# Channel scale and bias of the recurrence's output norm taken into the neighbouring operations

## The chip, the cores and the metric

The kernel runs on one core of a Trainium2 chip. The metric is the device time of one execution in microseconds. Several executions of the kernel before were timed; the profile shows one further execution.

## The reference, cut to what matters

The reference is a network of two layers. Each layer has a first feed-forward block, a mixer with three branches (a linear recurrence, a global and a windowed attention) and a second feed-forward block, on 256 tokens of 1024 channels, all in 32-bit floats. The change lies at the end of the recurrence's branch. There the sum `wkv` of the recurrence's two directions is normalized per head of 64 channels, scaled and shifted per channel, a bonus is added, and the result is multiplied with a gate:

```
mean = jnp.mean(wkv, axis=-1, keepdims=True)
var = jnp.mean(jnp.square(wkv - mean), axis=-1, keepdims=True)
y = ((wkv - mean) * lax.rsqrt(var + LNX_EPS)).reshape(bsz, s, RWKV_DIM) * lnx_g + lnx_b
y = y + bonus.reshape(bsz, s, RWKV_DIM)
gate = jax.nn.sigmoid(gl) @ g2
return y * gate
```

There are 8 heads of 64 channels, so 512 channels, and `lnx_g` and `lnx_b` have one value for each of them.

## The kernel before

One core does everything. Every weight matrix streams from HBM in units of 128x1024 floats (`unit`). Each unit is split into a high part `w_hi` (a rounding copy, line 62 on ScalarE or line 64 on VectorE) and a low part `w_lo` (a subtraction, line 93 on VectorE or GpSimd), and TensorE multiplies high with high, high with low and low with high (`mm3`, line 52). So nearly all of TensorE's time goes to weight matmuls, and the other engines work ahead of it.

The mixer consists of generators that each do a piece of work and then yield: the projections, the attention, the preparation of the recurrence, its four units (`wkv`, two halves of the heads by two directions), `post` and the output projections with their gates (`branches`). A string `ORDER`, written out by hand, tells which generator takes the next step; its letter O is `post`. Within this order the tile framework fills the queue of each engine. Another set of strings (`ENG`) picks the engine of single operations; the one for O is eight times v, VectorE.

`post` works on channels across partitions: a half of the heads is a tile `y` (`yacc`) of 128 channels by 2 pairs (`pp`) by 256 tokens, so 128x512. For each of the two halves it takes three steps. The first forms the product for the bonus (lines 974 and 975) and subtracts the mean (line 979). The second forms 1/rms per head and token (`head_rsqrt`: line 693 on VectorE, 694 on GpSimd, 696 on ScalarE). The third, which the change touches, spreads 1/rms over the channels with transposes into a PSUM bank `rb` (`hb` in the profile), multiplies `y` with it (line 985), applies the channel scale and bias from the columns `R_LG` and `R_LB` of the tile `par` (line 988, once for each `pp`), forms the bonus in a bank `bb` (`bonp`) and the gate in a bank `gb` (`gatep`) on TensorE, and then does on VectorE lines 995 (bonus times v), 996 (y plus bonus) and 997 (times gate). `split` follows: line 128 on ScalarE writes the high part of `yT`, line 130 on VectorE the low part. The output projection `wo` (lines 1044 and 1045 add its result up) multiplies with both parts. It comes soon after the third step of the second half; after that of the first half the units of the recurrence go on.

Of the kernel before, what the change touches and what calls it, by code (L numbers as in the profile page):

```python
# [11 lines left out]
ALU = mybir.AluOpType  # L12
# [16 lines left out]
class Net:  # L29
# [21 lines left out]
    def mm(self, *a, **k):  # L51
        return self.nc.tensor.matmul(*a, **k)  # L52
# [286 lines left out]
R_MU, R_W0, R_A0, R_KK, R_KA, R_RK, R_LG, R_LB, R_N = 0, 15, 23, 31, 35, 39, 43, 47, 51  # L339
# [16 lines left out]
class Mixer:  # L356
# [606 lines left out]
    def post(self):  # L963
        nc, n = self.nc, self.n
        V, mm = nc.vector, n.mm
        for hf in range(2):
            y, kas = self.ys[hf], self.unit[2 * hf][3]
            ps = slice(2 * hf, 2 * hf + 2)
            r, k, v = (self.RKV[:, i, ps, :] for i in range(3))
            pz = self.t([128, 4, 512], "pz", tag="Z", bufs=2)  # L970
            sq, bon = (pz[:, i].rearrange("p (a s) -> p a s", a=2) for i in (0, 1))
            for pp in range(2):
                p = 2 * hf + pp
                V.scalar_tensor_tensor(bon[:, pp, :], r[:, pp, :], self.par[:, R_RK + p:R_RK + p + 1], k[:, pp, :], ALU.mult, ALU.mult)
            self.pick("O").tensor_tensor(bon, bon, kas, ALU.mult)
            b = n.bank([128, 2, S], "mean")
            for pp in range(2):
                mm(b[:, pp, :], n.bones, y[:, pp, :], start=True, stop=True)
            V.tensor_tensor(y, y, b, ALU.subtract)
            nc.scalar.activation(sq, y, AF.Square)  # L980
            yield
            rb = self.head_rsqrt(sq, 2, 1.0 / 64, 64 * 1e-5, False, pz[:, 2])
            yield
            rb = rb()[0]
            V.tensor_tensor(y, y, rb, ALU.mult)
            for pp in range(2):
                p = 2 * hf + pp
                self.pick("O").tensor_scalar(y[:, pp, :], y[:, pp, :], self.par[:, R_LG + p:R_LG + p + 1], self.par[:, R_LB + p:R_LB + p + 1], ALU.mult, ALU.add)
            bb = n.bank([128, 2, S], "bonp")
            gb = n.bank([128, 2, S], "gatep")  # L990
            for pp in range(2):
                p = 2 * hf + pp
                mm(bb[:, pp, :], n.bones, bon[:, pp, :], start=True, stop=True)
                mm(gb[:, pp, :], self.g2[:, 128 * p:128 * p + 128], self.LG[:, 2, :], start=True, stop=True)
            V.scalar_tensor_tensor(bon, bb, 64.0, v, ALU.mult, ALU.mult)
            self.pick("O").tensor_tensor(y, y, bon, ALU.add)
            V.tensor_tensor(y, y, gb, ALU.mult)
            if hf == 0:
                self.ya = [self.t([128, 4, S], f"yT{i}", tag=f"yT{i}", bufs=2, dt=F32R) for i in range(2)]
            n.split(y, self.ya[0][:, ps, :], self.ya[1][:, ps, :])  # L1000
            yield
# [129 lines left out]
```

## Time and profile before

| what | us |
|---|---|
| median of 3 runs | 1452.02 |
| lowest and highest of them | 1450.62, 1454.06 |
| the profiled execution | 1456.31 |
| its span in the profile | 1454.4 |
| TensorE (PE) busy in the span | 1401.1 |
| VectorE (DVE) busy | 1004.6 |
| ScalarE (ACT) busy | 744.4 |
| GpSimd (POOL) busy | 206.2 |

PEld is the weight load of TensorE, which overlaps its matmuls. A line such as L93 is a line of the kernel. In the profile an operation reads as output<-inputs by the names of the tiles, with the shapes of the output and of the input that it goes over. A DVE instruction can start a little before the one ahead of it has ended, so distances between starts are shorter than durations where nothing has to be waited for.

### The profile page before, as it was taken

The page shows a single profiled execution, that of the slowest core. Times are in us where ns is not written, and L with a number is a line of the kernel's source. Part 1 is how long each engine was busy: PE and PEld are TensorE (multiplying, and loading weights), DVE is VectorE, ACT ScalarE, POOL GpSimd, SP SyncE. Part 2 cuts the span into 40 slices and gives each one's busy share as a digit, 9 for nine tenths or more (in the row PEclk, how much of TensorE's full clock was granted, in tenths as well). Part 3 has the DMA queues.
Part 4 walks back from the last instruction along what each step waited for, and adds up shares of the span by engine and source line. Part 5 has one row for each costly group of instructions (what it writes and reads, how often), then busy time and mean ns, then how long its engine had stood idle before and what let it go on. Part 6 is the DMA issues. An engine that isn't in the chain of part 4 may idle for free.

```text
span 1454.4 us, 25957 instructions
## 1 busy us (share of the span) xinstructions
PE 1401.1 (96%) x10482; PEld 1158.6 (80%) x10482; DVE 1004.6 (69%) x1518; ACT 744.4 (51%) x1241; POOL 206.2 (14%) x181
## 2 busy tenths in 40 slices
PE   7999999999998999999999999999998989999997
PEld 6888878877786878888888888788676868788886
DVE  5677467886867576776467864789758766668753
ACT  6555334665444355555455553356553443655543
POOL 0000033104315100000000000522041241000001
PEclk9999999999999999999999999999999999999999
DMA  7766656423314047666566666563243131576663
GB/s 219 209 201 187 195 152 190 130 70 120 113 50 144 27 144 205 189 191 194 162 188 196 190 192 191 159 182 100 67 132 102 49 114 48 167 207 188 189 191 112
DMA packets 113436, 220.24 MB, mean 151 GB/s; under 512 B 7362, under 2 KB 32164, under 8 KB 113316
## 3 DMA queue, kind: packets, MB, share of 16 engines
q1 hardware_dynamic: 111328, 215.08, 49.4%
q10 hardware_dynamic: 1508, 2.58, 0.5%
q8 instruction: 82, 1.34, 0.4%
q0 software_dynamic: 480, 0.93, 0.3%
q14 instruction: 38, 0.31, 0.1%
HBM read 217.51 MB, written 1.05 MB: 150 GB/s over the span
## 4 chain that ended last, share of the span: by engine, by line
PE 74%; DVE 8%; issue 8%; ACT 4%; DMA 3%; POOL 3%; SPq 0%; POOLq 0%; ACTq 0%; DVEq 0%
PE dn L52 19%; PE gt L52 18%; PE up L52 17%; PE gu L52 3%; PE wo L52 3%; PE rk L52 3%; DVE w_lo L93 2%; DMA w_raw<-in_w_in 2%; PE yp L52 1%; POOL w_lo L93 1%; PE Lp L52 1%; PE tp L55 1%; PE sc L52 1%; ACT w_hi L62 1%; DMA w_raw<-in_ffn_w_up 1%
## 5 line engine op out<-in xcount | busy, mean ns | idle before, releaser
L93 DVE TENSOR_TENSOR w_lo<-w_raw,w_hi 128x1024 fp32r<-128x1024 f32 (+1 forms) x360 | 444.1, 1234 | 252.0 <-ACT w_hi L62 248.5
L62 ACT ACTIVATE w_hi<-w_raw 128x1024 fp32r<-128x1024 f32 x358 | 379.8, 1062 | 403.4 <-PE dn L52 118.6
L52 PE MATMUL dn<-w_hi,aT 128*128 128x512 f32 x704 | 218.2, 390 | 0.0
L52 PE MATMUL gt<-hT,w_hi 128*128 128x512 f32 x512 | 179.0, 395 | 0.0
L52 PE MATMUL up<-hT,w_hi 128*128 128x512 f32 x512 | 178.2, 394 | 0.0
L52 PEld LDWEIGHTS dn<-w_hi,aT 128*128 128x128 f32 x704 | 131.9, 188 | 27.9 <-DVE sg L268 0.9
L93 POOL TENSOR_TENSOR w_lo<-w_raw,w_hi 128x1024 fp32r<-128x1024 f32 x50 | 123.5, 2474 | 149.4 <-ACT w_hi L62 91.1
L52 PE MATMUL gt<-hT,w_lo 128*128 128x256 f32 x512 | 142.2, 278 | 0.0
L52 PE MATMUL up<-hT,w_lo 128*128 128x256 f32 x512 | 141.8, 277 | 0.0
L52 PE MATMUL gt<-w_hi,hT 128*128 128x512 f32 x384 | 138.3, 421 | 0.0
L52 PE MATMUL dn<-w_lo,aT 128*128 128x512 f32 x352 | 137.7, 391 | 0.0
L52 PEld LDWEIGHTS up<-hT,w_hi 128*128 128x128 f32 x512 | 96.0, 188 | 22.3
L52 PEld LDWEIGHTS gt<-hT,w_hi 128*128 128x128 f32 x512 | 96.0, 188 | 22.1
L52 PEld LDWEIGHTS gt<-hT,w_lo 128*128 128x128 f32 x512 | 96.1, 188 | 0.2
L52 PEld LDWEIGHTS up<-hT,w_lo 128*128 128x128 f32 x512 | 96.1, 188 | 0.0
L52 PE MATMUL rk<-hT,w_hi 128*128 128x256 f32 x480 | 89.8, 288 | 4.0 <-DVE RKV L675 4.0
L52 PEld LDWEIGHTS gt<-w_hi,hT 128*128 128x128 f32 x384 | 73.0, 194 | 20.6 <-issue 5.2
L52 PEld LDWEIGHTS rk<-hT,w_hi 128*128 128x128 f32 x480 | 76.5, 194 | 6.9 <-DVE RKV L675 5.9
L52 PE MATMUL up<-w_hi,hT 128*128 128x512 f32 x256 | 81.4, 397 | 0.0
L52 PE MATMUL gt<-w_lo,hT 128*128 128x512 f32 x192 | 79.0, 411 | 0.0
L52 PEld LDWEIGHTS dn<-w_lo,aT 128*128 128x128 f32 x352 | 66.1, 188 | 14.8 <-DVE w_lo L93 1.4
L143 POOL TENSOR_SCALAR stat<-stat 128x1 f32<-128x1 f32 x14 | 3.4, 240 | 495.1 <-ACT gh L139 478.7
(272 smaller groups left out, 2427.9 us busy)
## 6 DMA issues: line engine op xcount, KB each, us to landing
w_raw<-in_ffn_w_up SPq DMA_DIRECT2D x160, 512.0 KB
w_raw<-in_w_in SPq DMA_DIRECT2D x102, 512.0 KB
w_raw<-in_ffn_w_down SPq DMA_DIRECT2D x88, 512.0 KB
w_raw<-in_ffn_w_up SPq DMA_DIRECT2D x32, 256.0 KB
w_raw<-in_w_out SPq DMA_DIRECT2D x16, 512.0 KB
w_raw<-in_w_o_ga SPq DMA_DIRECT2D x8, 512.0 KB
w_raw<-in_w_o_wa SPq DMA_DIRECT2D x8, 512.0 KB
w_raw<-in_w_o_rwkv SPq DMA_DIRECT2D x8, 512.0 KB
```

The costliest lines, as they stand in the source:

```text
L52: return self.nc.tensor.matmul(*a, **k)
L55: return self.nc.tensor.transpose(*a, **k)
L62: self.nc.scalar.activation(out, in_, AF.Copy, scale=1.0 if scale is None else scale)
L93: self.engine(on[1]).tensor_tensor(o, r, h.bitcast(F32), ALU.subtract)
L143: nc.gpsimd.tensor_scalar(self.ss[:, c:c + 1], self.ss[:, c:c + 1], 1.0 / D, EPS, ALU.mult, ALU.add)
```

## The change

The operation that multiplied the whole tile with 1/rms becomes two, one for each `pp`, which multiply with the channel's scale first and then with 1/rms. The bias is no longer added with the scale: the operation that added the bonus to the whole tile becomes two, which add the channel's bias and the bonus. The two operations of line 988 fall away. All new operations are on VectorE.

```
-            V.tensor_tensor(y, y, rb, ALU.mult)
             for pp in range(2):
                 p = 2 * hf + pp
-                self.pick("O").tensor_scalar(y[:, pp, :], y[:, pp, :], self.par[:, R_LG + p:R_LG + p + 1], self.par[:, R_LB + p:R_LB + p + 1], ALU.mult, ALU.add)
+                V.scalar_tensor_tensor(y[:, pp, :], y[:, pp, :], self.par[:, R_LG + p:R_LG + p + 1], rb[:, pp, :], ALU.mult, ALU.mult)
             bb = n.bank([128, 2, S], "bonp")
             gb = n.bank([128, 2, S], "gatep")
             for pp in range(2):
...
                 mm(bb[:, pp, :], n.bones, bon[:, pp, :], start=True, stop=True)
                 mm(gb[:, pp, :], self.g2[:, 128 * p:128 * p + 128], self.LG[:, 2, :], start=True, stop=True)
             V.scalar_tensor_tensor(bon, bb, 64.0, v, ALU.mult, ALU.mult)
-            self.pick("O").tensor_tensor(y, y, bon, ALU.add)
+            for pp in range(2):
+                p = 2 * hf + pp
+                V.scalar_tensor_tensor(y[:, pp, :], y[:, pp, :], self.par[:, R_LB + p:R_LB + p + 1], bon[:, pp, :], ALU.add, ALU.add)
             V.tensor_tensor(y, y, gb, ALU.mult)
```

## Rows read from the trace of the kernel before

**Rows 1.** Page, busy us, share of the span, instructions of an engine.
```profile
PE 1401.1 (96%) x10482; PEld 1158.6 (80%) x10482; DVE 1004.6 (69%) x1518; ACT 744.4 (51%) x1241; POOL 206.2 (14%) x181
```

**Rows 2.** Page, the chain that ended last, share of the span by engine.
```profile
PE 74%; DVE 8%; issue 8%; ACT 4%; DMA 3%; POOL 3%; SPq 0%; POOLq 0%; ACTq 0%; DVEq 0%
```

**Rows 3.** Groups by line and form, DVE: busy us, mean ns, idle before.
```profile
L675 DVE SCALAR_TENSOR_TENSOR RKV<-rk,par,projpad 128x256 f32<-128x256 f32 x24 | 11.3, 477 | 0.0
...
L974 DVE SCALAR_TENSOR_TENSOR pz<-RKV,par 128x256 f32<-128x256 f32 x8 | 3.5, 482 | 2.7 <-PE y L52 2.7
...
L988 DVE TENSOR_SCALAR yacc<-yacc,par 128x256 f32<-128x256 f32 x8 | 2.9, 408 | 0.1
...
L996 DVE TENSOR_TENSOR yacc<-yacc,pz 128x512 f32<-128x512 f32 x4 | 2.8, 693 | 0.1
...
L985 DVE TENSOR_TENSOR yacc<-yacc,hb 128x512 f32<-128x512 f32 x4 | 2.8, 688 | 7.4 <-PE hb L55 7.4
```

**Rows 4.** Timeline, DVE, layer 1, second half: start, us, operation, idle before.
```profile
505.82 0.69 DVE L985 TENSOR_TENSOR yacc<-yacc,hb 128x512 f32<-128x512 f32 x1 [3.19 <-PE hb L55]
506.54 0.73 DVE L988 TENSOR_SCALAR yacc<-yacc,par 128x256 f32<-128x256 f32 x2
507.19 0.68 DVE L995 SCALAR_TENSOR_TENSOR pz<-bonp,RKV 128x512 f32<-128x512 f32 x1
507.91 0.69 DVE L996 TENSOR_TENSOR yacc<-yacc,pz 128x512 f32<-128x512 f32 x1
508.71 0.69 DVE L997 TENSOR_TENSOR yacc<-yacc,gatep 128x512 f32<-128x512 f32 x1
509.31 1.22 DVE L93 TENSOR_TENSOR w_lo<-w_raw,w_hi 128x1024 fp32r<-128x1024 f32 x1
510.45 0.68 DVE L130 TENSOR_TENSOR yT<-yacc,yT 128x512 fp32r<-128x512 f32 x1
```

**Rows 5.** Timeline, ACT, layer 1, second half.
```profile
507.94 1.06 ACT L62 ACTIVATE w_hi<-w_raw 128x1024 fp32r<-128x1024 f32 x1 [2.94 <-PE wo L52]
509.43 0.63 ACT L128 ACTIVATE yT<-yacc 128x512 fp32r<-128x512 f32 x1 [0.43 <-DVE yacc L997]
```

**Rows 6.** Timelines, PE and PEld, layer 1, second half.
```profile
506.41 0.59 PE L52 MATMUL bonp<-pz,consts 128*128 128x256 f32 x2
...
510.12 0.19 PEld L52 LDWEIGHTS wo<-w_hi,yT 128*128 128x128 f32 x1 [0.33 <-ACT yT L128]
```

**Rows 7.** Timeline, DVE, layer 1, first step of the first half.
```profile
414.08 0.88 DVE L974 SCALAR_TENSOR_TENSOR pz<-RKV,par 128x256 f32<-128x256 f32 x2 [0.71 <-PE y L52]
```

**Rows 8.** Timeline, DVE, layer 1, third step of the first half.
```profile
472.80 0.69 DVE L985 TENSOR_TENSOR yacc<-yacc,hb 128x512 f32<-128x512 f32 x1 [0.50 <-PE hb L55]
474.51 0.69 DVE L995 SCALAR_TENSOR_TENSOR pz<-bonp,RKV 128x512 f32<-128x512 f32 x1 [1.02 <-PE bonp L52]
475.11 0.73 DVE L988 TENSOR_SCALAR yacc<-yacc,par 128x256 f32<-128x256 f32 x2
475.87 0.69 DVE L996 TENSOR_TENSOR yacc<-yacc,pz 128x512 f32<-128x512 f32 x1
476.67 0.69 DVE L997 TENSOR_TENSOR yacc<-yacc,gatep 128x512 f32<-128x512 f32 x1
478.79 0.68 DVE L64 COPY Zt<-T 64x512 f32<-64x512 f32 x1 [1.43 <-ACT Zt L62]
```

**Rows 9.** Timeline, PE, layer 1, around the third step of the first half.
```profile
470.83 0.32 PE L52 MATMUL tp<-sol,Tn 32*32 32x32 f32 x13 [1.83 <-issue]
...
472.55 1.91 PE L52 MATMUL bonp<-pz,consts 128*128 128x256 f32 x4
```

**Rows 10.** Windows there: us, busy of PE, PEld, DVE, ACT, POOL, granted clock, DMA.
```profile
472.00:474.00 2.00, 2.00 (x9) 1.73 (x7) 0.98 (x2) 1.44 (x4) 0.00 (x0) 0.50 0.35 141
474.00:476.00 2.00, 2.00 (x8) 1.41 (x6) 1.46 (x4) 0.00 (x0) 0.00 (x0) 0.76 0.00 0
```

More of the change, by code (lines that the diff above doesn't have):

```diff
@@ L984, in post @@
             rb = rb()[0]
-            V.tensor_tensor(y, y, rb, ALU.mult)
             for pp in range(2):
                 p = 2 * hf + pp
-                self.pick("O").tensor_scalar(y[:, pp, :], y[:, pp, :], self.par[:, R_LG + p:R_LG + p + 1], self.par[:, R_LB + p:R_LB + p + 1], ALU.mult, ALU.add)
+                V.scalar_tensor_tensor(y[:, pp, :], y[:, pp, :], self.par[:, R_LG + p:R_LG + p + 1], rb[:, pp, :], ALU.mult, ALU.mult)
             bb = n.bank([128, 2, S], "bonp")
@@ L995, in post @@
             V.scalar_tensor_tensor(bon, bb, 64.0, v, ALU.mult, ALU.mult)
-            self.pick("O").tensor_tensor(y, y, bon, ALU.add)
+            for pp in range(2):
+                p = 2 * hf + pp
+                V.scalar_tensor_tensor(y[:, pp, :], y[:, pp, :], self.par[:, R_LB + p:R_LB + p + 1], bon[:, pp, :], ALU.add, ALU.add)
             V.tensor_tensor(y, y, gb, ALU.mult)
```

## The prediction

> **What bounds the kernel now.** I read the page first: busy times, then the chain that ended last, then DVE's groups by form, and last the timelines of the four places where the changed step runs. TensorE is busy for 96% of the span and VectorE for 69% [rows 1], and the chain that ended last runs 74% of the way over PE and 8% over DVE [rows 2]. So DVE time counts only where PE stands still for it. The changed step, the third piece of `post`, runs four times, for two halves of the heads in each of two layers. The profiled execution took 1456.31 us, 1.91 more than its span of 1454.4; the median of the runs shown, 1452.02, is 4.29 below it. I work the sum as a difference on the profiled execution and put it on the median.
>
> **What goes and what comes.** A half loses one TENSOR_TENSOR of 128x512 (688 ns), two TENSOR_SCALAR of 128x256 (408 each) and one TENSOR_TENSOR of 128x512 (693): 2197 ns [rows 3]. It gains two SCALAR_TENSOR_TENSOR of 128x256 with one PSUM operand and a column scale, for which line 675 is the same form but for the operand that lies in PSUM (477 ns), and two from SBUF alone, which line 974 is exactly (482 ns): 1918 ns [rows 3]. That is 279 ns less busy time per half, 1.1 us in all. Instructions stay six per half (1+2+1+1+1 against 2+1+2+1, with lines 995 and 997 kept). No matmul, DMA or POOL instruction changes, and no queue of SP or POOL is passed. The engine list for "O" is all v, so the picks that fall away shift nothing to another engine.
>
> The Trainium skill, "VectorE: DVE Perf Modes", section "Rules for kernel authors", says not to fuse chained DVE operations for speed, since the pipeline is drained after each one anyway, and to cut their number instead. By that rule alone six for six would save nothing, where the rows give 1.1 us. No run here tests it yet, and the answer below is the same either way.
>
> **Second halves, where PE waits.** Here the DVE order is 985, 988, 988, 995, 996, 997 [rows 4]. Line 997 starts at 508.71; ACT's line 128 waits for it (0.43 us idle) and starts at 509.43; and PE's next weight load, at 510.12, had idled 0.33 us for ACT [rows 5, 6]. So a delay of 997 reaches PE in full, while an earlier 997 gives back at most 0.33 us per layer.
>
> Now the same stretch after the change. The two operations that read the 1/rms bank start at 505.82, as 985 does, and as a pair take 0.88 us (line 974's pair of 414.08 [rows 7]), so they are done at 506.70. Today 985 and the two of 988 fill the engine until 507.19. But line 995 cannot start at 506.70: its operand is the bonus product, whose last matmuls end at 506.41 + 0.59 = 507.00 [rows 6]. In the first half the bonus matmuls end at 472.55 + 1.91 = 474.46 and 995 starts at 474.51, 0.05 later [rows 8, 9]; so here 995 starts at 507.05, 0.14 earlier than now and not 0.49. The next dependent operation follows 0.72 later, as 996 follows 995 (507.19 to 507.91 [rows 4]): 507.77. Then comes what the change puts in place of 996's 0.69: a pair of 0.88. From 996's end (508.60) to 997's start is 0.11 now; with it 997 starts at 507.77 + 0.88 + 0.11 = 508.76. That is 0.05 later than now: the 0.14 gained before the bonus is spent by the dearer add after it, which is 0.19 longer. Two layers: +0.1 us.
>
> Bounds: if neither operation of the pair overlaps the other (2 x 0.482 = 0.96, plus a dependent step's 0.03), 997 comes 0.16 later than now, +0.3 us in all. Below nothing: if 997 came earlier by all the 279 ns that a half saves, as it would were the bonus product there in time, PE would get back 0.28 of its 0.33 us in each layer: -0.6 us. I take the worked value, +0.1, since each step of it has a row.
>
> **First halves, which are covered.** Here the queue runs 985, 995, 988, 988, 996, 997: line 995 stands before 988 and DVE idles 1.02 us there for the bonus matmuls [rows 8]. After the change the pair ends at 472.80 + 0.88 = 473.68, 995 still waits until 474.51, the second pair starts at 475.23 and ends at 476.11, and 997 starts at 476.22 where it now starts at 476.67. That is 0.45 us earlier, and nobody wants it: the next DVE instruction waits for ACT until 478.79 in any case (1.43 us idle [rows 8]). That idle time is the cover; without it the gain would be 0.45 us per layer. The 1/rms bank comes free 0.19 us later (473.68 for 473.49), with nothing in the listing that comes up short: DVE itself idles until 474.51 right behind it. Price: 0.
>
> **Sum.** +0.1 us on 1452.02: 1452.1. Even if all the removed busy time lay on the path it would be 1452.02 - 1.1 = 1450.9. What a measurement of this kernel tells from no change is about 0.2%, 2.9 us; the three runs themselves span 3.4 us. So with the order of the queues unchanged the time is the same whichever price is right, and only a different order can bring it out of that bound. That the order can differ is in the rows: 995 runs ahead of 988 in the first halves and behind it in the second, so the queues are filled by a plan with times of its own, not in program order.
>
> **Rival 1, slower: the plan puts a weight split ahead of line 997.** In the second half DVE runs line 93 (1.22 us) directly behind 997 [rows 4]. It could go from 509.00 on, when ACT's copy of the same unit ends (507.94 + 1.06 [rows 5]), 0.29 after 997's start. If 997 becomes ready later than that, by the plan's reckoning, the split goes first, and it decides from there: 997 starts at 509.00 + 1.14 (the distance from line 93 at 509.31 to the next at 510.45 [rows 4]) = 510.14, 1.43 later, and PE stands still as long. Two layers: +2.9, 1454.9. A gap of that kind may also bring the clock down: in the first half PE idled 1.83 us before 470.83 and was then granted 0.50 in 472 to 474 and 0.76 in 474 to 476 [rows 9, 10], the lower of its two levels (1.2 for 2.4 GHz) for part of the time; 2 x 0.50 + 2 x 0.24 = 1.5 us lost. With that, +5.9: 1457.9. For it: only 0.29 us separate the two now, and my estimate moves 997 the wrong way by 0.05. Against it: the plan's modelled times are not in the trace, and with fewer elements to work through it may as well see 997 earlier. Chance 0.15.
>
> **Rival 2, faster: the plan closes the gap in the first halves.** The 1.83 us of idle PE and the 1.5 us lost at the lower clock behind it, 3.3 per layer, lie just ahead of the step. If the new plan places the 1/rms transposes, the bonus matmuls or gate matmuls so that they fill it, up to 6.6 us come back, and I take half: 1448.7. Against it: the gap is set by what runs on DVE ahead of line 985, which the change does not touch. Chance 0.15.
>
> **The change doesn't do what it says** (the fused operations cost as much as what they replace): DVE's 1.1 us stay, and the total is 1452.0. That is within the forecast.
>
> **How the numbers follow.** Forecast, 0.70: 1452.1, own range 1449.4 to 1454.0 (the -1.1 and +0.3 of the prices, and 1.7 for half the spread of the runs). Rival 1 has 0.15 with 1454.9 to 1457.9, rival 2 has 0.15 around 1448.7. The range 1448.5 to 1455.5 takes in the near half of each and leaves out at most 2 in 10. Faster by over 0.2% is rival 2, slower rival 1: 0.15, 0.70, 0.15.
>
> **What would show it.** Right: the four new operations at 470 to 490 ns; in the second halves 995 starting right behind the last bonus matmuls, and 997 within 0.2 us of its old distance from the 1/rms transposes; ACT's line 128 still the last thing PE waits for; DVE busy 1.1 us less; first halves' DVE idle behind 997 longer. Wrong: a line 93 between the 1/rms operations and 997; a different order of PE's gate, bonus and transposing matmuls around either half; a different granted clock behind the first half's gap; or fused operations over 550 ns, with which the second halves would be late by more than the 0.29 us that keep line 93 behind.

## The result and the profile after

The changed kernel takes 1459.81 us (median of 9 runs, 1456.23 to 1469.65) where the kernel before took 1452.49 (9 runs, 1443.64 to 1456.23) on the same chip. The ratio is 1.0054, with a 95% interval of [1.0034, 1.0074]: slower by half a per cent, 7.3 us by the medians. The forecast was 1452.1, with a range from 1448.5 to 1455.5. The profiled execution of the changed kernel took 1458.13 us, with a span of 1456.2.

The page of the changed kernel, busy times and the chain that ended last, which answer to [rows 1, 2]:

```profile
PE 1399.7 (96%) x10482; PEld 1158.3 (80%) x10482; DVE 1004.4 (69%) x1518; ACT 744.0 (51%) x1241; POOL 205.1 (14%) x181
...
PE 80%; DVE 10%; ACT 4%; issue 2%; POOL 2%; DMA 2%; SPq 0%; POOLq 0%; DVEq 0%; ACTq 0%
```

No engine has more work than before, and the numbers of instructions are the same, so busy time cannot tell where the microseconds went; the chain still runs over TensorE, and somewhat more over VectorE (10% for 8%). The operations cost what they were priced at. The groups by line and form of the changed kernel, DVE (answering to [rows 3]; line 987 multiplies with scale and 1/rms, 994 forms the bonus, 997 adds bias and bonus, 998 is the gate):

```profile
L997 DVE SCALAR_TENSOR_TENSOR yacc<-yacc,par,pz 128x256 f32<-128x256 f32 x8 | 3.5, 482 | 0.1
L987 DVE SCALAR_TENSOR_TENSOR yacc<-yacc,par,hb 128x256 f32<-128x256 f32 x8 | 3.5, 477 | 7.5 <-PE hb L55 7.5
L994 DVE SCALAR_TENSOR_TENSOR pz<-bonp,RKV 128x512 f32<-128x512 f32 x4 | 2.8, 690 | 0.8 <-PE bonp L52 0.7
```

These are the 477 and 482 ns of the forecast to the nanosecond. What differs is the order in the queues. Laid side by side, the two kernels' queues agree except around the changed step in each layer. In the second half VectorE now runs this (the timeline of the changed kernel, DVE, layer 1; the answer to [rows 4]):

```profile
501.23 0.69 DVE L960 TENSOR_TENSOR yacc<-yacc,y 128x512 f32<-128x512 f32 x1 [1.09 <-PE y L52]
...
505.64 0.17 DVE L693 TENSOR_SCALAR hss<-hs 128x8 f32<-128x8 f32 x1 [1.81 <-PE hs L52]
509.81 0.87 DVE L987 SCALAR_TENSOR_TENSOR yacc<-yacc,par,hb 128x256 f32<-128x256 f32 x2 [4.00 <-PE hb L55]
510.60 1.22 DVE L93 TENSOR_TENSOR w_lo<-w_raw,w_hi 128x1024 fp32r<-128x1024 f32 x1
511.92 0.69 DVE L994 SCALAR_TENSOR_TENSOR pz<-bonp,RKV 128x512 f32<-128x512 f32 x1
512.65 0.88 DVE L997 SCALAR_TENSOR_TENSOR yacc<-yacc,par,pz 128x256 f32<-128x256 f32 x2
513.63 0.69 DVE L998 TENSOR_TENSOR yacc<-yacc,gatep 128x512 f32<-128x512 f32 x1
```

A weight split, line 93, stands between the 1/rms pair and the bonus. And VectorE has idled 4.00 us for the transposes, not 3.19. One reason is that GpSimd too runs a split first (POOL, same place, the changed kernel and then the kernel before):

```profile
503.91 2.38 POOL L93 TENSOR_TENSOR w_lo<-w_raw,w_hi 128x1024 fp32r<-128x1024 f32 x1 [35.12 <-ACT w_hi L62]
506.25 1.63 POOL L694 TENSOR_TENSOR hss<-hss,stat 128x8 f32<-128x8 f32 x1
```
```profile
502.70 1.64 POOL L694 TENSOR_TENSOR hss<-hss,stat 128x8 f32<-128x8 f32 x1 [35.41 <-DVE hss L693]
504.31 2.35 POOL L93 TENSOR_TENSOR w_lo<-w_raw,w_hi 128x1024 fp32r<-128x1024 f32 x1
```

Line 694, the power for 1/rms, is wanted at 505.64 + 0.17 = 505.81 but stands behind the split until 506.25; before, it started 0.08 us after line 693 had ended. TensorE runs dry for 1.72 us, for 0.67 before, and then works at the lower clock, so that its four transposes take 1.11 us for 0.66 (PE, the kernel before and then the changed one, and windows of the latter with us, busy of PE, PEld, DVE, ACT and POOL, granted clock, DMA share and GB/s):

```profile
505.06 0.66 PE L55 MATMUL hb<-head,pz 128*128 128x128 f32 x4 [0.67 <-ACT pz L696]
```
```profile
508.59 1.11 PE L55 MATMUL hb<-head,pz 128*128 128x128 f32 x4 [1.72 <-ACT pz L696]
509.50 1.06 PE L52 MATMUL bonp<-pz,consts 128*128 128x256 f32 x2
```
```profile
508.00:510.00 2.00, 1.41 (x6) 1.32 (x7) 0.19 (x1) 1.49 (x2) 0.00 (x0) 0.50 0.53 215
510.00:512.00 2.00, 2.00 (x9) 1.64 (x7) 1.90 (x4) 0.00 (x0) 0.00 (x0) 0.66 0.00 0
```

The 0.36 us of the later power and the 0.45 of the slower transposes are what VectorE waits longer in layer 1. In layer 2 the clock stayed up, and it waits 3.54 us.

A third split got ahead of the addition whose result TensorE transposes next. VectorE and TensorE, changed kernel, layer 1:

```profile
520.50 1.21 DVE L93 TENSOR_TENSOR w_lo<-w_raw,w_hi 128x1024 fp32r<-128x1024 f32 x1
521.63 0.68 DVE L1046 TENSOR_TENSOR merged<-merged,tha 128x512 f32<-128x512 f32 x1
```
```profile
522.46 0.74 PE L55 MATMUL tp<-head,merged 128*128 128x128 f32 x5 [1.12 <-DVE merged L1046]
```

With the new operations in the old order (first experiment) that wait is 0.24 us.

To follow this through the experiments I use two stretches of each layer. The first runs from the start of the last doubling step of the recurrence's units ahead of the first half's 1/rms pair (line 871 on VectorE) to the second half's last recurrence addition (line 960). The second runs from there to the first residual update (line 201). Windows over both, layer 2, columns as above. Kernel before, then changed:

```profile
1191.41:1217.79 26.38, 26.38 (x539) 23.18 (x540) 18.29 (x38) 11.04 (x23) 0.00 (x0) 0.94 0.14 43
1217.79:1253.02 35.23, 34.34 (x160) 27.22 (x160) 21.77 (x29) 14.37 (x18) 6.17 (x3) 1.00 0.41 119
```
```profile
1191.78:1218.64 26.86, 26.70 (x545) 23.19 (x546) 17.88 (x38) 10.91 (x23) 0.00 (x0) 1.00 0.13 41
1218.64:1254.75 36.11, 32.79 (x154) 26.18 (x154) 21.96 (x29) 14.47 (x18) 5.28 (x3) 1.00 0.39 117
```

The counts tell a fourth thing: TensorE runs six matmuls more in the first stretch (545 for 539) and six fewer in the second (154 for 160), and there it stands idle 36.11 - 32.79 = 3.32 us where it stood idle 0.89. The six are gate matmuls (`gt`). They stood behind the recurrence's mean, where TensorE would otherwise wait; now they stand ahead in the first stretch, which TensorE fills anyway. The first stretch looks hardly longer here, but only because before was granted 0.94 of the clock in it and after 1.00; at equal clock the difference is 2 us, as the experiments show.

### The profile page after: what moved, and what is told of

The parts are those of the page before. It is cut to its first block, busy times and chain, and to the rows that moved or that the text cites. A ratio compares the mean times of both kernels' runs of the same rounds, so it can differ in the third digit from the quotient of the medians.

```text
span 1456.2 us, 25956 instructions
## 1 busy us (share of the span) xinstructions
PE 1399.7 (96%) x10482; PEld 1158.3 (80%) x10482; DVE 1004.4 (69%) x1518; ACT 744.0 (51%) x1241; POOL 205.1 (14%) x181
## 4 chain that ended last, share of the span: by engine, by line
PE 80%; DVE 10%; ACT 4%; issue 2%; POOL 2%; DMA 2%; SPq 0%; POOLq 0%; DVEq 0%; ACTq 0%
PE dn L52 19%; PE gt L52 19%; PE up L52 18%; PE gu L52 3%; PE rk L52 3%; PE wo L52 2%; PE pj L52 2%; PE yp L52 1%; PE tp L55 1%; DVE w_lo L93 1%; DMA w_raw<-in_w_in 1%; PE tx L52 1%; PE Lp L52 1%; PE rm L52 1%; PE y L52 1%
```

## The experiments

Two theories at first: the order of the queues costs the time (the operations being as priced), or the operations do, in a way that the rows don't show. Each kernel below states an order of its own: a helper, given here in short, takes the instructions of the engines in the order wanted and tells the framework to issue them so. In the traces e1 has the order of before on every engine, and e2 that of the changed kernel. The helper adds no waits and no work.

```
+def pinned(tc, orders):          # called behind network(tc, a, out)
+    had = {i.name: i for i in tc.nc.cur_bb.bb.instructions}
+    for names in orders:         # one list for each engine and stretch
...
+            if last:
+                tc.add_manual_dep(had[name], last, mybir.DependencyInfo(mybir.DependencyClass.NoSync, mybir.DependencyReason.DATA), reason="pinned")
+            last = name
```

All were timed against the kernel before on the same chip. Stretches are from the timelines of each profiled execution, layer 1 / layer 2, with the granted clock where it isn't 1.00. In layer 2 of e1, e4, e6, e11 and e12 the last two doubling steps run back to back, where elsewhere the second waits 0.5 to 1.6 us for TensorE. A timeline can show such a pair as one row; the stretch starts at the second of the two, as in the others:

| kernel | ratio to before | first stretch, us | second stretch, us |
|---|---|---|---|
| before | 1 | 26.40 (0.94) / 26.38 (0.94) | 35.25 / 35.23 |
| changed | 1.0054 [1.0034, 1.0074] | 28.51 (0.94) / 26.86 | 36.91 (0.95) / 36.11 |
| e1 new operations, old order | 1.0011 [0.9999, 1.0023] | 26.19 (0.94) / 24.60 | 35.29 / 35.29 |
| e2 old operations, new order | 1.0064 [1.0044, 1.0083] | 28.47 (0.94) / 26.86 | 36.49 / 36.49 |
| e3 first halves in old order | 1.0064 [1.0043, 1.0084] | 26.39 (0.94) / 27.40 (0.90) | 40.55 (0.92) / 40.66 (0.92) |
| e4 second halves in old order | 1.0021 [1.0004, 1.0037] | 28.52 (0.94) / 26.69 | 34.82 / 34.85 |
| e5 VectorE's split back | 1.0039 [1.0022, 1.0055] | 28.53 (0.94) / 28.50 (0.94) | 36.95 (0.95) / 35.56 |
| e6 GpSimd's power first | 1.0035 [1.0016, 1.0054] | 26.86 / 26.70 | 35.77 / 35.74 |
| e7 six gate matmuls back | 1.0019 [1.0001, 1.0037] | 26.87 / 26.86 | 35.27 / 35.26 |
| e8 bonus matmuls early | 0.9983 [0.9967, 1.0000] | 26.38 (0.94) / 24.72 | 34.29 / 34.33 |
| e9 as e4, VectorE's copies first | 1.0039 [1.0023, 1.0055] | 26.80 / 26.81 | 34.86 / 34.84 |
| e10 as e9, bonus early | 1.0010 [0.9995, 1.0025] | 26.87 / 26.81 | 33.85 / 33.86 |
| e11 old operations in e8's order | 0.9999 [0.9982, 1.0016] | 26.39 (0.94) / 24.55 | 34.58 / 34.57 |
| e12 three gate matmuls early | 0.9997 [0.9983, 1.0012] | 26.96 (0.94) / 25.56 | 34.84 / 34.83 |

In one and the same order the first stretch takes 1.4 to 1.8 us more at 0.94 of the clock than at 1.00, so stretches are compared at one clock.

**Order or operations.** e1 has the changed operations in the order of before, e2 the operations of before in the order of the changed kernel:

```
# e1: kernel after, e2: kernel before
 network(tc, a, out)
+pinned(tc, ORDER_OF_BEFORE)     # e1
+pinned(tc, ORDER_OF_AFTER)      # e2
```

> The changed operations, with every engine's queue put back into the order that it had before the change (the four new operations stand where the four old ones stood). Theory A, the loss is the order alone: 1452.5 us, within 0.2% of before, since in that order only the small gain and loss of the operations are left (+0.1 us by the prediction, -1.1 at most). Theory B, the fused operations themselves delay the output projection: still slower by 0.4% or more, 1458 to 1461.

> The operations of before, with every engine's queue in the order that it has after the change. Theory A, the order: slower by 0.4 to 0.7%, 1458 to 1462 us, though no operation is changed. Theory B, the operations: the same as before, 1452.5 within 0.2%.

The order decides. With the old order the changed kernel takes 1451.67 us for 1450.75 before, within what the measurement tells; with the new order the old operations are as late as the changed kernel (1459.81). VectorE's second half in e1, layer 1:

```profile
503.87 0.87 DVE L987 SCALAR_TENSOR_TENSOR yacc<-yacc,par,hb 128x256 f32<-128x256 f32 x2 [3.19 <-PE hb L55]
505.10 0.69 DVE L994 SCALAR_TENSOR_TENSOR pz<-bonp,RKV 128x512 f32<-128x512 f32 x1 [0.36 <-PE bonp L52]
505.83 0.88 DVE L997 SCALAR_TENSOR_TENSOR yacc<-yacc,par,pz 128x256 f32<-128x256 f32 x2
506.81 0.69 DVE L998 TENSOR_TENSOR yacc<-yacc,gatep 128x512 f32<-128x512 f32 x1
```

The bonus starts 1.23 us after the 1/rms pair and the gate 2.94 us after it. The prediction had 507.05 - 505.82 = 1.23 and 508.76 - 505.82 = 2.94.

**One half at a time.** The changed kernel with the old order on all engines around the first halves only (e3), or around the second halves only (e4):

```
+pinned(tc, FIRST_HALVES_OF_BEFORE)    # e3, second halves as changed
+pinned(tc, SECOND_HALVES_OF_BEFORE)   # e4, first halves as changed
```

> The changed operations; the queues stand as before the change around the first half of the step and up to the mean of the second, and as after the change from there to the output projection. If the loss is shared by both places, as in the profile of layer 1 (2.1 us before the second half's first operation, 1.7 behind it): +0.25%, about 1456. If it is all in the second half (the weight split ahead of the bonus, GpSimd's weight split ahead of its power): +0.5%, 1459 to 1460. If it is all in the first: within 0.2% of before.

> The changed operations; the queues stand as after the change around the first half of the step, where a weight's copy and split go ahead on VectorE and gate matmuls go earlier on TensorE, and as before the change in the second half. Shared loss: +0.25%, about 1456. All in the second half: within 0.2% of before. All in the first: 1459 to 1460.

e4 brings the second stretch to 34.8 and leaves 2 us in the first one, so both halves cost. e3 does not answer its question. Its first stretch is back in layer 1 (layer 2 was granted 0.90 of the clock), but the second grows to 40.6: the new second half lets ScalarE read the gate matmuls (`tha` and `kd`) ahead of the mean square (line 980), and the old first half leaves six of those matmuls behind the mean. So line 980 starts 4.74 us after line 960, for 2.63 in the changed kernel. The two halves of an order belong together.

**The two splits of the second half.** e5 is the changed kernel with VectorE's split behind the gate, e6 with GpSimd's power ahead of its split:

```
 VectorE, second half (e5)
-L987 L987 L93 L994 L997 L997 L998
+L987 L987 L994 L997 L997 L998 L93
 GpSimd, second half (e6)
-L93 L694
+L694 L93
```

> The changed kernel in its own order, but on VectorE the weight split that stands between the 1/rms operations and the bonus of the second halves goes behind the gate's multiplication, as before the change. If that split is what makes the second halves late (it takes 1.22 us, and the bonus started 1.92 us behind the first 1/rms operation in layer 2, 1.23 us in the old order): the bonus 0.7 us nearer, and the stretch from the recurrence's last addition to the first residual update 36.1 becomes 35.4 us per layer; the whole 1.4 us less than the changed kernel, +0.4% against before. If the split only fills a wait for the bonus matmuls: less than 0.1 us per layer.

> The changed kernel in its own order, but on GpSimd the power for 1/rms goes ahead of the weight split, as before the change. If that split makes 1/rms late: the 1/rms transposes 0.36 us nearer to the recurrence's last addition (7.00 for 7.36), the stretch up to the first residual update shorter by as much, the whole 0.7 us less than the changed kernel; more, up to 1.2 us per layer, if TensorE's gap ahead of the transposes is then short enough for the clock to stay high. If not: no change in that stretch.

At full clock the second stretch goes from 36.11 to 35.56 in e5 and to 35.74 in e6: VectorE's split costs 0.55 us there and GpSimd's 0.37. In layer 1 of e5 the gain is nothing (36.95 for 36.91): there the bonus matmuls ran at the lower clock, as after the change, and the split had hidden behind them. With GpSimd's power first both layers kept the full clock in that stretch. That is one profile, so it is not shown that e6 always does. The whole runs of e5 and e6 can't be told from that of the changed kernel, whose interval they overlap.

**What the first halves lose by.** These things differ there: six gate matmuls come earlier on TensorE, which also runs some of the units' products (`lv`) ahead of transposes that came first before; ScalarE copies a `Tn` later; and VectorE runs a weight unit's copy and split ahead of the units' copies. e7 has the old second halves and moves six gate matmuls back behind the mean:

```
 TensorE, first halves (e7), gate matmuls only
-... gt x18, tx, ..., gt x4, mean, ...
+... gt x16, tx, ..., mean, gt x6, ...
```

> The changed operations; second halves in the old order; first halves in the new one, but for six gate matmuls (1.4 us of TensorE) that go back behind the mean of the second half, where they stood before the change. If it is these matmuls, run early where TensorE is already busy, that lengthen the first halves (28.5 us from the units' second doubling step to the recurrence's last addition, 26.4 before): 27.1, and the second stretch 35.25 as before; the whole within 0.2% of before. If it is VectorE's weight copy and split ahead of the units' copies: 28.5 stays, and with 35.25 behind it the whole is +0.25%, 1454 to 1456.

The first stretch stays at 26.87. I took that for evidence against the gate matmuls, and it was a flaw of the experiment: what had to be moved stood in two places, and the old order has 12 of the 22 ahead of the units' second run of products (`tx`), and e7 still has 16. So e9, again with the old second halves, does the opposite, and puts VectorE's copy and split back with TensorE and ScalarE left in the new order:

```
 VectorE, first halves (e9, e10)
-COPY TT | CAST w_hi | L93 w_lo | COPY Tn | COPY Zt x3 | COPY TT | COPY Zt
+COPY TT | COPY Tn | COPY Zt x3 | COPY TT | COPY Zt | CAST w_hi | L93 w_lo
```

> The changed operations; second halves in the order of before on every engine; first halves in the changed kernel's order on TensorE and ScalarE, while VectorE alone goes back to the order of before (the weight unit's cast and split stand behind the units' copies again). Theory VectorE's early weight split: the stretch from the units' last doubling step to the second half's last recurrence addition goes back to 24.7 to 24.9 us at the full clock (26.2 to 26.4 at 0.94) in both layers, the stretch behind it is 34.8 to 35.3 us, and the whole stands at 0.9995 to 1.001 of the kernel before. Theory TensorE's order: the first stretch stays at 26.9 (28.5 at the lower clock), and the whole stays near 1.002, as with the second halves alone put back.

26.8: VectorE's early split is not what holds the stretch there, and my theory of that moment falls. (Its whole, 1.0039, lies above e4's 1.0021, though the stretches of the two agree to 0.1 us where the clock is the same; their intervals overlap.) What holds it shows in TensorE's timeline. First e1, then e9, both at full clock in layer 2 (the units' doubling step began at 1186.49 in e1 and at 1192.73 in e9):

```profile
1186.72 0.63 PE L55 MATMUL hb<-head,pz 128*128 128x128 f32 x4
...
1198.05 0.50 PE L52 MATMUL gt<-w_lo,hT 128*128 128x512 f32 x1
1198.39 0.62 PE L52 MATMUL gt<-w_hi,hT 128*128 128x512 f32 x2
1198.85 0.40 PE L52 MATMUL gt<-w_lo,hT 128*128 128x512 f32 x1
1199.18 0.32 PE L52 MATMUL tx<-Zt,TT 64*64 64x128 f32 x1
```
```profile
1193.16 0.60 PE L55 MATMUL hb<-head,pz 128*128 128x128 f32 x4
...
1206.22 0.72 PE L52 MATMUL gt<-w_hi,hT 128*128 128x512 f32 x2
1206.78 0.39 PE L52 MATMUL gt<-w_lo,hT 128*128 128x512 f32 x1
1207.01 0.61 PE L52 MATMUL gt<-w_hi,hT 128*128 128x512 f32 x2
1207.46 0.39 PE L52 MATMUL gt<-w_lo,hT 128*128 128x512 f32 x1
1207.78 0.32 PE L52 MATMUL tx<-Zt,TT 64*64 64x128 f32 x1
```

The products start 12.69 us after the doubling step in e1 and 15.05 in e9, and TensorE idles for no more than 0.16 us of e9's whole stretch (the window below). e12 tests it by dose: the changed operations in the old order, with three of the six gate matmuls moved ahead.

```
 TensorE, first halves (e12), gate matmuls only
-... gt x12, tx, ..., gt x4, mean, gt x6, ...
+... gt x15, tx, ..., gt x4, mean, gt x3, ...
```

> The changed operations in the order of before on every engine, except that in each first half three of the six gate matmuls that stand behind the recurrence's mean are put ahead of the units' second run of product matmuls (the changed kernel's order has six more there). If each gate matmul put ahead of the units' chain delays it by its own time, the stretch from the units' last doubling step to the second half's last recurrence addition is 25.6 to 25.9 us at the full clock (24.7 to 24.9 with none moved, 26.8 to 26.9 with six), some 27.2 at the lower clock; ScalarE's mean-square operation behind it starts 2.64 us after that addition in place of 3.10 (it no longer waits for the gate matmuls), so the second stretch is 34.8 to 35.3 us; the whole is 0.2 to 1.2 us over the same kernel with none moved, 1.000 to 1.002 of before. The rival, that the loss comes from ScalarE's later copies or from the interleaving of the units' matmuls: the first stretch stays at 24.7 to 24.9 (26.2 to 26.4).

None, three and six gate matmuls ahead give 24.60, 25.56 and 26.81 us at full clock: 0.32 us for each of the first three and 0.42 for each of the next. (What was expected of e12 went by 24.93 for none moved, read from the first of e1's two steps.) Windows over the first stretch of e1, e12 and e9, layer 2, and TensorE in e12:

```profile
1186.49:1211.09 24.60, 24.53 (x538) 21.56 (x538) 17.80 (x40) 11.62 (x24) 0.00 (x0) 1.00 0.18 57
```
```profile
1184.09:1209.65 25.56, 25.42 (x542) 22.28 (x543) 17.97 (x40) 11.74 (x24) 0.00 (x0) 1.00 0.18 57
```
```profile
1192.73:1219.54 26.81, 26.65 (x545) 23.16 (x546) 17.96 (x39) 10.70 (x22) 0.00 (x0) 1.00 0.14 41
```
```profile
1184.52 0.60 PE L55 MATMUL hb<-head,pz 128*128 128x128 f32 x4
...
1196.02 0.50 PE L52 MATMUL gt<-w_lo,hT 128*128 128x512 f32 x1
...
1197.85 0.32 PE L52 MATMUL tx<-Zt,TT 64*64 64x128 f32 x1
```

Counted from the first half's transposes (`hb`), the stretches are 24.37, 25.13 and 26.38 us, so 0.25 us for each of the first three and 0.42 for each of the next. The first three cost about their own length: the four matmuls ahead of the products take 1199.18 - 1198.05 = 1.13 us in e1, and the seven in e12 1197.85 - 1196.02 = 1.83, so 0.23 each. e9 has more than three matmuls beyond e12, namely the rest of the new order on TensorE and ScalarE. At e12's price six matmuls make 1.5 to 1.9 of its 2.0 to 2.2 us; what remains probably goes with that rest, which no kernel moved alone.

The matmuls give some of it back: with three or six moved, line 980 starts 2.64 us after line 960, where it starts 3.10 after it in the old order since ScalarE waits for a gate matmul ahead of it; the second stretch is 34.84 for 35.29. The whole of e12 cannot be told from before, nor should it be, with 1 us lost and 0.45 given back in each layer.

By that dose e7, with four ahead, should stand at 24.60 + 3 x 0.32 + 0.42 = 25.98 us, and it stands at 26.86. In e7 VectorE's copy of `lv` for the products starts 13.97 us after the doubling step, behind the early split, against 13.60 in e9. So the early split probably holds the stretch as well once TensorE doesn't; a kernel with that alone was not tried.

**A better order.** In e1 VectorE idles 0.36 us for the bonus, while the bonus needs nothing of 1/rms. e8 is e1 with the bonus and gate matmuls, and the bonus operation, put right behind the recurrence's last head sums in the second halves:

```
+            if hf == 0:
                 rb = rb()[0]
                 for pp in range(2): ...      # y * scale * 1/rms
             bb = n.bank([128, 2, S], "bonp")
...
             V.scalar_tensor_tensor(bon, bb, 64.0, v, ALU.mult, ALU.mult)
+            if hf:
+                rb = rb()[0]
+                for pp in range(2): ...      # y * scale * 1/rms
```

> The changed operations in the old order, but in the second halves the bonus and gate matmuls and the bonus' multiplication run right behind the sums for 1/rms, where VectorE has idled 3.2 us and TensorE 0.67 us, and not behind the 1/rms transposes. If the chain of the step sets the stretch: the gate's multiplication at 10.1 us behind the recurrence's last addition for 11.17, TensorE's idle 0.67 and 0.33 us gone, the stretch up to the first residual update 34.3 to 34.6 us per layer for 35.29, the whole 1.4 to 2 us under before (-0.1%). If the output projection's matmuls set it: 35.3 stays.

VectorE in e8, second half, layer 2 (here 995 is the bonus, 1000 the 1/rms pair, 1003 the pair that adds, 1004 the gate):

```profile
1218.89 0.69 DVE L995 SCALAR_TENSOR_TENSOR pz<-bonp,RKV 128x512 f32<-128x512 f32 x1 [1.24 <-PE bonp L52]
1220.85 0.87 DVE L1000 SCALAR_TENSOR_TENSOR yacc<-yacc,par,hb 128x256 f32<-128x256 f32 x2 [1.27 <-PE hb L55]
1221.64 0.87 DVE L1003 SCALAR_TENSOR_TENSOR yacc<-yacc,par,pz 128x256 f32<-128x256 f32 x2
1222.54 0.69 DVE L1004 TENSOR_TENSOR yacc<-yacc,gatep 128x512 f32<-128x512 f32 x1
```

The bonus is done in what was idle time, and the gate starts 9.92 us after line 960, for 11.16 in e1. The second stretch falls by 1.0 us in each layer, to 34.3. Of that, 0.66 is TensorE's wait for ScalarE ahead of the 1/rms transposes, which the moved matmuls fill (PE, layer 2, e1 and then e8):

```profile
1218.55 0.66 PE L55 MATMUL hb<-head,pz 128*128 128x128 f32 x4 [0.66 <-ACT pz L696]
```
```profile
1217.31 0.68 PE L52 MATMUL bonp<-pz,consts 128*128 128x256 f32 x2
...
1220.08 0.66 PE L55 MATMUL hb<-head,pz 128*128 128x128 f32 x4
```

The other 0.3 is about what the weight load behind ScalarE's line 128 had idled (0.37 us in e1, hardly any in e8). e8 is the fastest kernel of the study, 1450.03 us for 1452.36 before, well below the changed kernel; that it beats the kernel before is at the edge of its interval.

e10 puts the same early bonus into e9; e11 asks what the fused operations add once the bonus is there in time:

```
 e10 = e9 + the early bonus of e8
 e11 = e8, with before's y*(1/rms), y*scale+bias, y+bonus in place of the two pairs
```

> As the kernel with VectorE's copies put first, and in the second halves the gate's and the bonus's matmuls and the bonus operation stand right behind the recurrence's last matmuls. If VectorE's early split is what the first halves lost by, the first stretch is 24.8 us at the full clock (26.4 at 0.94) and the second one at most 34.3; the whole is 1.0 to 2.5 us below the kernel before (0.998 to 0.9993). The rival, that TensorE's order is what costs: the first stretch 26.9, the second 34.3, and the whole some 1.0015 of before.

> The operations of the kernel before in the order of the kernel with the early bonus matmuls. It asks whether the six fused operations are worth their 0.28 us per half once the bonus is there in time. If they are, the gate product starts 10.2 us behind the recurrence's last addition (9.93 with the fused operations), the first residual update at 34.6 (34.3), and the whole is 0.3 to 0.6 us above that kernel, 0.9985 to 0.9995 of before. The rival: the time is as with the fused operations, since something other than VectorE's chain sets the residual update; then 34.3.

e10's second stretch is shorter by the same 1.0 us (33.85), and its first one keeps the 26.8 of TensorE's new order: the rival written down for it. In e11 the gate starts at 10.45 us, 0.52 after e8's, more than the 0.28 by which the single durations differ: the two operations of a pair overlap (0.87 us for 2 x 0.48), and the second pair starts before the first has ended; at the residual update 0.26 is left (34.57 for 34.31). So there the fusion is worth a quarter of a microsecond a layer. The whole times, 0.9999 and 0.9983 with intervals that overlap, do not confirm more than that.

## Why the prediction was wrong

**What goes and what comes: right.** The four operations took 477 and 482 ns. The Trainium skill's rule, "VectorE: DVE Perf Modes", section "Rules for kernel authors", that fusing chained operations wins nothing, was set beside it; here the groups that went had 2.9 + 2.8 + 2.8 = 8.5 us [rows 3], the new ones have 7.0 with as many instructions, and VectorE is busy 1003.1 us in e1 for 1004.6. So for the busy time of these forms the rows hold, and the rule doesn't; the whole times do not tell the two apart. The 1.5 us are more than the 1.1 of the forecast, which added single durations where the operations of a pair overlap. (In the changed kernel itself the page total fell by 0.2 only; 0.7 came back in two additions of line 1046, one a layer, which took 1.12 and 0.97 us for 0.68 and ran beside an addition of GpSimd's.)

**Second halves, in the old order: right to 0.01 us** in both distances (e1). Its bound of 0.33 us a layer for an earlier gate is not contradicted either: e8 gave back 1.0, but 0.66 of it by filling TensorE's wait ahead of the transposes, with matmuls that the change does not move. What is left, 0.3, is of the bound's size. A bound for other orders has to be read from the whole stretch, where TensorE was idle 35.23 - 34.34 = 0.89 us before.

**First halves: right.** The cover held: in e1 VectorE still waited for ScalarE behind the gate, 1.60 us in layer 1, and the whole was the same.

**The sum: this is the step that failed.** It said that "with the order of the queues unchanged the time is the same", which held (e1, 1.0011), and gave 0.70 to the order staying, so that a new order stood in its sum with nothing, while the rows it quoted showed queues filled by a plan with times of its own. The plan was made anew, and moved work on all four engines. From e1 to the changed kernel, layer 2 at full clock, the two stretches grow from 24.60 + 35.29 = 59.89 to 26.86 + 36.11 = 62.97, by 3.08 us. TensorE's and ScalarE's new order in the first halves, six gate matmuls ahead above all, costs 2.21 in the first stretch and gives back 0.45 in the second (e9); GpSimd's split costs 0.37 (e6) and VectorE's 0.55 (e5); that makes 2.68. The other 0.40 probably lies behind them, where TensorE waits 0.98 us in layer 2 for line 1046 behind its split, for 0.23 in e1; no kernel moved that split alone. Two layers make 6.2 us, and the ratios of 1.0011 and 1.0054 are as far apart, though their intervals leave room for some microseconds. Layer 1 of the profiled execution lost more, with the second stretch at 36.91 for 36.11, at the lower clock behind the 1.72 us gap.

**Rival 1 was the right kind in the wrong place.** It put a split between line 996 and 997 for 1.43 us a layer. The split went between the 1/rms pair and the bonus, where the wait for the bonus hid part of it (0.55), and the costlier move, the gate matmuls, stood only in the list of what would show the forecast wrong, with no price. Its remark on the clock came true in layer 1. **Rival 2** asked for a plan that closes the gap ahead of the first half. The changed kernel still has it, with 1.83 us in layer 1 and 1.11 in layer 2. The order alone does not set it: e1, in the order of before, has 1.13 in layer 1 and none above 0.1 in layer 2, where before had 1.83 and 1.54.

**Open:** why the plan moved just these. The framework's reckoning is not in the trace. That the new operations set it off follows from the diff having nothing else; which of its times tipped it was not tried.

## What to carry to other kernels

Where a framework plans the queues, a change of a few instructions is two changes, and here the second, the new order, was the whole of the loss as far as these runs can tell: compare the queues before looking at prices, and pin the old order to measure the operations alone. Filler work belongs where the bounding engine would wait; moved to where it is busy, the three matmuls of e12 cost about their whole length. And an experiment that undoes a move has to be counted in the new trace, for a move that is only half undone looks like a wrong theory.

## What the hardware showed besides

The same idle time does not bring the same clock. In the changed kernel TensorE idled 1.72 us ahead of the second half's transposes in both layers; the four took 1.11 us in layer 1, where the windows grant 0.50, the lower of the two levels, and 0.66 in layer 2, at 1.00. In e8 TensorE idled 1.92 us ahead of the first half in layer 1 and 1.68 in layer 2; the first stretch was granted 0.94 and took 26.38 us, the other 1.00 and 24.72. The two profiled executions agree in their spans to 2 us (1454.4 before and 1456.2 after) where the medians are 7.3 apart; before was granted 0.94 in the first stretch of both layers, after only in layer 1.
